# Where the weights lie in SBUF against the activations: a 64-byte gap, and a first chunk split by single row blocks

## The chip, the core and the metric

The kernel runs on one core of one Trainium2 chip, in one launch. The metric is device time in microseconds. Three runs of the kernel before gave 2261.34, 2262.07 and 2262.89 us; the median is 2262.07. All arrays are float32, 517 MB of them pass through the DMA queues, nearly all weights that are read once.

## What is computed

Two transformer blocks on 256 tokens of width 2048, shortened to what fills the time:

```python
# block 1
proj = rms_norm(x, mix_norm) @ w_in                 # 2048 x 5128
h = x + concat([forgetting_attention(q, k, v, log_f), gelu(rg) * rg_lru(conv(rx))]) @ w_out
hn = rms_norm(h, ffn_norm)                          # top-1 group of 4, then top-2 of its 8 experts
for e in range(32):
    out += (silu(hn @ w_gate[e]) * (hn @ w_up[e])) @ w_down[e] * comb[:, e]
h = h + out
h = h + sigmoid(rms_norm(h, ple_norm) @ w_ple_gate) * (p @ w_ple_up)
# block 2
h = h + concat([diff_attention, moba_attention, dilated_attention]) @ w_out_2   # after h @ w_in_2, 2048 x 6144
h = h + memory_cross_attention(rms_norm(h, g_cross), rms_norm(mem, g_mem))
h = h + (silu(conv(rms_norm(h, g_ffn) @ w_up[:, :5632])) * (.. @ w_up[:, 5632:])) @ w_down
return rms_norm(h, g_final)
```

## The kernel before

**Products.** A dense product is computed as three products in the type float32r: weights and activations are each split into a high part (rounded to float32r) and a low part (the rest), and high x high, high x low and low x high are summed in PSUM. `mm` (line 506) issues every one of them. Two forms exist. In `form_a` a 128x128 block of weights is stationary and 256 columns of activations (all tokens) move past it; in `form_b` a 128x128 block of activations is stationary and up to 512 columns of weights move. Form A does `w_in`, `w_out`, the gated per-layer input, `w_in_2`, `w_out_2` and `w_up` (tiles `xth/xtl`, `oth/otl`, `xtph/xtpl`, `xt2h/xt2l`, `ot2h/ot2l`, `xtuh/xtul`, and `xm`, `xtc`, `om` of the memory attention); form B does the values' columns and `w_down` (`hs`).

**The weight stream.** `plan` cuts each weight matrix into units of at most 1 MB, which go by DMA from the SP queue into one of five raw tiles (`raw`). A unit is split in quarters of 1024 columns in a row (`quarters`): ScalarE copies a quarter to a `hi` tile (`split_hi`), VectorE subtracts to a `lo` tile (`split_lo`). There are four `hi` and four `lo` tiles, used in turn; a quarter has its `hi` and its `lo` at the same place in the turn. `next_quarter` takes the next pair, and the loops of `form_a` or `form_b` issue its products: 24 of 256 columns, or 12 of 512. A chunk of 512 output columns is eight quarters. The first chunk (`w_in` from column 3072, 520 wide) differs: a unit there has two row blocks of 520 columns and is one quarter of 1040; its eight columns of the forget gate are a fifth block, so a row block has 15 products and the other blocks start 8 columns into the row.

**The order.** Each engine takes its instructions in the order of emission. Work beside the products (evacuations, attention, norms, splits) is cut into tasks, and a model of the engines' clocks (`clk`, `pump`) picks the step that can start first. It knows no addresses.

**The experts** run on a buffer scheme of their own: their weights are used unsplit, as float32, from raw tiles, from three slots and from the `hi` and `lo` tiles. `gather` (line 1343) multiplies the tokens in rows (`xnh`, `xnl`) by a one-hot tile `gq`; `combine` multiplies the experts' outputs `yy` by a one-hot tile `gt`. Both move the one-hot tile, and both issue 512 products of 256 columns.

**Where tiles lie.** The tile pools are laid one behind the other in a partition in the order in which they are opened, each tile at a multiple of 32 bytes. Before:

| pool | holds | bytes per partition | starts at | modulo 256 |
|---|---|---|---|---|
| `per` | `h`, `ident`, small tiles | 25632 | 16512 | 128 |
| `slots` | six slots: all activation operands | 6 x 16384 | 42144 | 160 |
| `stm` | five `raw` of 8320 | 41600 | 140448 | 160, 32, 160, 32, 160 |
| | four `hi` of 4160 | 16640 | 182048 | 32, 96, 160, 224 |
| | four `lo` of 4160 | 16640 | 198688 | 32, 96, 160, 224 |
| `wk` | six work tiles of 2048, one-hot tiles and `pth`, `ptl` among them | 12288 | 215328 | 32 |
| `sm` | small tiles | | 227616 | |

A tile of 1040 float32 takes 4160 bytes, 64 more than a multiple of 256, so the four `hi` tiles lie at four different residues, and the `lo` tiles at the same four. The allocator hands them out in the order 0, 3, 2, 1, 0, and so on. A row block inside a tile starts a multiple of 512 bytes further (2080 in the first chunk), a block of activations a multiple of 1024: neither changes the residue, but for the first chunk.

Of the kernel before, what the change touches and what calls it, by code (L numbers as in the profile page):

```python
# [30 lines left out]
def block_kernel(ctx: ExitStack, tc: tile.TileContext, A, out, stop=None, dbg=None, force_general=False):  # L31
# [3 lines left out]
    per = ctx.enter_context(tc.tile_pool(name="per", bufs=1))  # L35
    slots = ctx.enter_context(tc.tile_pool(name="slots", bufs=1))
    stm = ctx.enter_context(tc.tile_pool(name="stm", bufs=3))
    wk = ctx.enter_context(tc.tile_pool(name="wk", bufs=1))
    sm = ctx.enter_context(tc.tile_pool(name="sm", bufs=8))
# [7 lines left out]
    # ------------------------------------------------------------------ order of emission  # L47
    # Every engine takes its instructions in the order in which they are emitted. Work beside the matrix products
    # is cut into tasks: generators that name the engine ("a", "d", "p") before each of their steps. A model of
    # the engines' clocks (us) picks the step that can start first, so that no engine waits for another one  # L50
    # inside a chain while it has other work.
# [18 lines left out]
    class Vec:  # L70
        def __getattr__(self, name):
            f = getattr(nc.vector, name)

            def g(o, *a, **k):
                f(o, *a, **k)  # L75
                ins = [x for x in a[:3] if not isinstance(x, (float, int)) and x is not None]
                fast = name in ("tensor_scalar", "tensor_copy", "memset") and all(x.space != PSM for x in ins)
                t = 0.068 + o.free_size() * (0.00052 if fast else 0.00104)
                if name == "tensor_reduce":
                    t = 0.068 + ins[0].free_size() * 0.00104  # L80
                if name in ("tensor_scalar", "scalar_tensor_tensor") and not isinstance(a[1], (float, int)):
                    t += 0.06
                now = clk["d"]
                # an operand that the last instruction has just written costs its latency
                w = last.get("o")
                if o.free_size() <= 64 and any(x.tensor is w for x in ins):
                    t += 0.13
                last["o"] = o.tensor
                clk["d"] = now + t
            return g  # L90
# [4 lines left out]
    def mul(o, l, r, start, stop):  # L95
        """a product beside the stream"""
# [66 lines left out]
    def advance(t):  # L163
        """run the task to its next request; False when it has ended"""
# [17 lines left out]
    def settle(t):  # L182
        """resolve conditions and delays; True when the task asks for an engine"""
# [39 lines left out]
    def candidates(qs):  # L223
        """[(start, priority, run it, engine)]"""
# [16 lines left out]
    def pump():  # L241
        """what fits beside the products that have been emitted"""
# [32 lines left out]
    # ------------------------------------------------------------------ weight stream  # L275
# [74 lines left out]
    for u, un in enumerate(units):  # L350
        if un["kind"] == "dense":
            un["nq"] = max(1, un["nkb"] * un["width"] // 1024)
# [9 lines left out]
    def raw_tile():  # L362
        return stm.tile([128, 4 * 520], F32, name="raw", tag="raw", bufs=RAWS)

    def hl_tiles(dtype):
        return (stm.tile([128, 1040], dtype, name="hi", tag="hi", bufs=HLS),
                stm.tile([128, 1040], dtype, name="lo", tag="lo", bufs=HLS))

    # buffers of the experts' weights: two slots in halves, the raw tiles, the tiles of the split weights, and
    # at first a third slot  # L370
# [13 lines left out]
    def exp_bufs(x):  # L384
        k, i = EBUF[x][0], int(EBUF[x][1])
        if k == "H":
            return [t[:, 0:1024] for t in hl_tiles(F32)], None
        if k == "R":
            t = raw_tile()[:, 0:2048]
# [31 lines left out]
    # the third slot is free after the raw tiles and most of the split weights' that come behind it  # L421
# [12 lines left out]
    def split_steps_open():  # L434
        """the steps of splitting that could be next: [(start, quarter, run it)]"""
# [35 lines left out]
    def next_quarter():  # L471
# [11 lines left out]
        if EXP0 - RAWS <= u < EXP0:  # L483
            # the first of the experts' weights, as tiles get free
# [12 lines left out]
    def need_of(done):  # L497
        """products wait until the blocks up to kb are there"""
# [9 lines left out]
    def form_a(X, kbs, blocks, first, last, need=None, beside=True):  # L508
        """W stationary: blocks = [(psum out [128, S], column, first in its bank)]"""
# [21 lines left out]
    def form_b(X, kbs, banks, first, last, width=512, need=None):  # L531
        """X stationary: banks[tt] psum [128, <=512]"""
# [37 lines left out]
    # ------------------------------------------------------------------ start: loads and constants  # L570
# [13 lines left out]
    # x and the first weights in turns; when they are there, about  # L584
# [16 lines left out]
    def warm(n):  # L601
        """products that nobody reads: the tensor engine's clock rises only after some us of work"""
# [16 lines left out]
    # the other constants, as rows to be transposed  # L619
# [30 lines left out]
    def const_gen():  # L650
# [19 lines left out]
        # half biases of the gates; 2 softplus(-lam), by atanh's series for log1p  # L670
# [37 lines left out]
    # ------------------------------------------------------------------ norms: sums over d, 1/rms per token  # L708
    def rsqrt(n, ssq, scale):
        """[128, n] 1/sqrt(ssq * scale + EPS)"""  # L710
# [18 lines left out]
    def have_r():  # L729
        """the condition that the norm asked for last is there"""  # L730
# [3 lines left out]
    def spread(r):  # L734
        """[128 tok, 2] per-token factors -> [128, 256] on all partitions, in PSUM"""
# [5 lines left out]
    def set_r(ssq, wide):  # L741
        """a task's steps: R["r"] [128 tok, 2] and R["b"] [128, 256] from sums of squares [128 tok, 2]"""
# [32 lines left out]
    def add_sq(sq, t):  # L775
        """the sum of the blocks' squares, by one more"""
# [6 lines left out]
    def operand(dst, kb, gain, sq, t, done):  # L783
        """a task's steps: block kb of h times the gain as an operand, and its squares"""
# [10 lines left out]
    def resid_gen(o, kb, dst, gain, sq, done):  # L795
        """h += o; operand of the next norm"""
# [4 lines left out]
    def split_steps(dst, kb, src, done=None):  # L801
        """a task's steps: an operand of src"""
# [19 lines left out]
    # ================================================================== block 1: mixing  # L822
# [49 lines left out]
    def bias_rows_gen():  # L872
        """relative-position bias of block 2, to DRAM:
        bias_d[head, q, c] = row[head, 127 - q + c], queries 128..255 at keys 0..255"""
# [31 lines left out]
    # minus the sums of log f, in three parts that add up to it exactly, at partitions 0, 32 and 64  # L906
# [61 lines left out]
    def rnn_gen():  # L968
        """scan; rc becomes the state.
        a = exp(-y), s = tanh(y/2): 1/(1+s) = (1+a)/2, refined; a = 2/(1+s) - 1; sqrt(1-a^2) = 2 sqrt(s)/(1+s)"""  # L970
# [27 lines left out]
    # F and RX  # L998
# [17 lines left out]
    # Q, K: per-head norms, transposed  # L1016
# [48 lines left out]
    # attention of block 1  # L1065
    def max_of(srcs, biases, p, m):
        """scores + bias -> p [128, 384], -max in m[2:4]"""
# [13 lines left out]
    def pt_steps(p):  # L1081
        """P [128 q, 384] -> P^T: [128 s0, 256 t] | [128 s1, 128 t]"""
# [11 lines left out]
    def pv_t(t, v, dst, kb, done=None):  # L1094
        """out^T [dh, tok] = V^T P^T, split into dst"""
# [46 lines left out]
    # RG: gelu(rg) * state  # L1142
# [27 lines left out]
    # w_out; tokens in rows for the experts; scores of the router  # L1170
# [33 lines left out]
    def xn_gen(n, tt):  # L1204
# [9 lines left out]
        if n == 3:  # L1214
            # beside the routing on the vector engine
# [46 lines left out]
    # ================================================================== block 1: experts  # L1262
# [22 lines left out]
    # groups of a token: [128, (tt), 4]; experts: [128, (tt, group), 8]. The choice does not depend on the token's  # L1285
    # 1/rms, a positive factor of all its scores; the first of equal ones is taken
# [31 lines left out]
    # place among the expert's tokens from 1 on where selected, 0 elsewhere  # L1318
# [17 lines left out]
    def gather(q):  # L1336
        """the tokens of four experts' slots: xe, by steps of two of its 16 rows"""
# [22 lines left out]
    def weights():  # L1360
        """weights of the two experts, times 1/rms of the token; what goes past the slots"""
# [39 lines left out]
    def loadable(u):  # L1401
        """whether the unit's buffer has been read"""
# [14 lines left out]
    def hidden(i):  # L1417
        """the experts' hidden values of pair i, times the slots' weights, and room for their transpose"""
# [42 lines left out]
    def transposes(i):  # L1461
        """of the hidden values, and of G"""
# [29 lines left out]
    # the first pair's hidden values beside its gather  # L1492
# [13 lines left out]
    for i in range(16):  # L1506
# [7 lines left out]
        if i == 15:  # L1514
            # p^T as an operand
# [9 lines left out]
        for j in range(2):  # L1525
# [16 lines left out]
            if i == 15:  # L1542
                # the next weights are split in time for the products that follow
# [27 lines left out]
    # general path: the tokens past an expert's slots, by dense products over all tokens  # L1571
# [54 lines left out]
    # ================================================================== block 1: gated per-layer input  # L1626
# [52 lines left out]
    # ================================================================== block 2: self attention  # L1679
# [134 lines left out]
    # w_out_2; the memory's operands beside it  # L1814
# [81 lines left out]
    # ================================================================== block 2: memory attention  # L1896
# [98 lines left out]
    # ================================================================== block 2: conv-GLU  # L1995
# [25 lines left out]
    def tok_gen():  # L2021
        """h in place to tokens in rows: h[p, kb, (tt, c)]"""
# [64 lines left out]
    # w_down: hid split as it is used; tokens in rows  # L2087
# [22 lines left out]
    def fin_gen(bank, n, tt):  # L2110
        """h += products (tokens in rows), sums of squares; times the final gain, but for the last columns"""
# [37 lines left out]
    def last_columns(X, banks):  # L2149
        """the last products of the last two column blocks, one token tile after the other"""  # L2150
# [40 lines left out]
def _constants():  # L2191
    """rows of a product with [bias table; ones; dilated heads]: distance d = 255 - i of column i"""
# [42 lines left out]
```

## Time and profile before

| | |
|---|---|
| median of three runs | 2262.07 us |
| profiled execution, span | 2260.5 us |
| TensorE busy | 2210.5 us (98%), 15552 products |
| weight loads of TensorE | 1887.0 us (83%) |
| VectorE busy | 1264.3 us (56%) |
| ScalarE busy | 943.7 us (42%) |
| DMA | 517.30 MB, 229 GB/s over the span, some 400 GB/s in the expert stage |
| granted clock of TensorE | 0.9 or more of full speed in 39 of 40 slices, 0.8 in the other |

The span is the time from the first to the last instruction of the profiled execution; the run's time has a little around it. A product's record is longer (0.28 us for 256 columns) than the distance to the next one's start, since products overlap in the pipeline; the pace of a stream is read from the starts. The stages, in order of time: block 1's mixing to about 395 us, experts to 905, the gated input to 1005, block 2's mixing to 1410, memory attention to 1520, `w_up` to 2005, `w_down` to the end.

### The profile page before, as it was taken

Reading aid. Unit: us, or ns where it says so; the run is one execution under the profiler, and the core shown is the slowest. Engines: PE = TensorE matmul, PEld = TensorE weight load, DVE = VectorE, ACT = ScalarE, POOL = GpSimd, SP = SyncE. Lnnn points to the kernel's source line nnn. Section 1 sums busy time; section 2 is a strip of 40 time slices with the busy share of each in tenths; the row PEclk is TensorE's granted clock in tenths of the full one; section 3 lists DMA queues with packets and bytes.
Section 4 is the critical chain, followed back from the end, with each engine's and each line's share of the span. In section 5 each row is a group of like instructions: output and inputs, shape, how many; then the busy total and the mean of one; then the engine's idle time right before and its main releaser. Section 6 shows DMA issues by size and latency. Waiting matters only on the chain.

```text
span 2260.5 us, 37736 instructions
## 1 busy us (share of the span) xinstructions
PE 2210.5 (98%) x15552; PEld 1887.0 (83%) x15552; DVE 1264.3 (56%) x2251; ACT 943.7 (42%) x1493; POOL 34.0 (2%) x62
## 2 busy tenths in 40 slices
PE   9999979999999999999999999999999999999998
PEld 8888978555455565998999999999999999988886
DVE  8866654233333334875477558675655665564545
ACT  6745533211111112654444446455444444444443
POOL 1000000000000000000000000000000000000000
PEclk9999989999999999999999999999999999999999
DMA  8554668999999997465545556555555565555552
GB/s 282 168 180 164 144 189 304 332 403 396 401 398 396 399 394 276 171 196 194 185 153 170 181 180 192 184 169 170 187 187 188 185 195 191 191 200 193 186 187 93
DMA packets 232415, 517.30 MB, mean 229 GB/s; under 512 B 11783, under 2 KB 51446, under 8 KB 232112
## 3 DMA queue, kind: packets, MB, share of 16 engines
q1 hardware_dynamic: 229168, 506.57, 63.7%
q0 software_dynamic: 3040, 8.27, 1.8%
q8 instruction: 124, 2.03, 0.4%
q14 instruction: 51, 0.42, 0.1%
q10 hardware_dynamic: 32, 0.01, 0.0%
HBM read 510.61 MB, written 4.19 MB: 228 GB/s over the span
## 4 chain that ended last, share of the span: by engine, by line
PE 59%; DVE 0%; ACT 0%; ACTq 0%; issue 0%
PE acc L506 51%; PE sd L506 6%; PE sd L97 2%; PE sd L699 1%; DVE rs L75 0%; DVE hid L75 0%; DVE lo L75 0%; ACT hi L61 0%; ACT junk L61 0%; ACT out L61 0%; DVE h L75 0%; ACT cx L61 0%; DVE hs L75 0%; ACTq L2231 0%; ACT xtph L61 0%
## 5 line engine op out<-in xcount | busy, mean ns | idle before, releaser
L75 DVE TENSOR_TENSOR lo<-raw,hi 128x1024 fp32r<-128x1024 f32 (+1 forms) x572 | 698.6, 1224 | 549.2 <-ACT hi L61 544.1
L61 ACT ACTIVATE hi<-raw 128x1024 fp32r<-128x1024 f32 (+1 forms) x572 | 605.6, 1059 | 768.8 <-PE acc L506 649.2
L506 PE MATMUL acc<-xtuh,hi 128*128 128x256 f32 x1408 | 393.9, 280 | 0.0
L506 PE MATMUL acc<-xtul,hi 128*128 128x256 f32 x1408 | 393.6, 280 | 0.0
L506 PE MATMUL acc<-xtuh,lo 128*128 128x256 f32 x1408 | 393.2, 279 | 0.0
L506 PEld LDWEIGHTS acc<-xtuh,lo 128*128 128x128 f32 x1408 | 266.1, 189 | 0.0
L506 PEld LDWEIGHTS acc<-xtuh,hi 128*128 128x128 f32 x1408 | 266.0, 189 | 0.0
L506 PEld LDWEIGHTS acc<-xtul,hi 128*128 128x128 f32 x1408 | 265.8, 189 | 0.0
L75 DVE TENSOR_TENSOR h<-acc,h 128x512 f32<-128x512 f32 (+1 forms) x180 | 101.7, 613 | 196.0 <-PE acc L506 196.0
L506 PE MATMUL acc<-xt2h,hi 128*128 128x256 f32 x512 | 147.5, 288 | 0.0
L506 PE MATMUL acc<-xt2l,hi 128*128 128x256 f32 x512 | 143.4, 280 | 0.0
L506 PE MATMUL acc<-xt2h,lo 128*128 128x256 f32 x512 | 143.4, 280 | 0.0
L506 PE MATMUL acc<-hi,hs 128*128 128x512 f32 x352 | 112.0, 393 | 0.8 <-ACT hs L61 0.7
L506 PE MATMUL sd<-hi,hs 128*128 128x512 f32 x352 | 111.7, 393 | 0.0
L61 ACT ACTIVATE sg<-acc,ws 128x256 f32<-128x256 f32 x16 | 7.6, 475 | 243.6 <-PE acc L1445 148.2
L506 PEld LDWEIGHTS acc<-xt2h,hi 128*128 128x128 f32 x512 | 96.8, 189 | 4.1 <-issue 4.0
L506 PEld LDWEIGHTS acc<-xt2l,hi 128*128 128x128 f32 x512 | 96.9, 189 | 0.1
L506 PEld LDWEIGHTS acc<-xt2h,lo 128*128 128x128 f32 x512 | 96.7, 189 | 0.0
L75 DVE TENSOR_TENSOR yy<-acc,yy 128x512 fp32r<-128x512 f32 x64 | 44.3, 692 | 92.4 <-ACT yy L61 92.4
L506 PEld LDWEIGHTS acc<-gt,yy 128*128 128x128 f32 x512 | 64.4, 188 | 30.4 <-issue 27.7
L506 PE MATMUL acc<-oth,lo 128*128 128x256 f32 x256 | 72.8, 284 | 12.3 <-DVE lo L75 12.3
L506 PEld LDWEIGHTS acc<-hi,hs 128*128 128x128 f32 x352 | 66.0, 188 | 16.4 <-ACT hs L61 0.9
(390 smaller groups left out, 4711.3 us busy)
## 6 DMA issues: line engine op xcount, KB each, us to landing
raw<-in_w_up_dram SPq DMA_DIRECT2D x88, 1024.0 KB, 5.0
raw<-in_w_in_dram SPq DMA_DIRECT2D x52, 1024.0 KB, 5.2
raw<-in_w_down_dram SPq DMA_DIRECT2D x44, 1024.0 KB, 5.0
raw<-in_w_out_dram SPq DMA_DIRECT2D x32, 1024.0 KB, 5.1
raw<-in_w_in_dram SPq DMA_DIRECT2D x64, 512.0 KB, 4.5
raw<-in_w_expert_down_dram SPq DMA_DIRECT2D x29, 1024.0 KB, 10.1
raw<-in_w_expert_gate_dram SPq DMA_DIRECT2D x45, 512.0 KB, 10.0
raw<-in_w_expert_up_dram SPq DMA_DIRECT2D x45, 512.0 KB, 10.2
```

The source lines that it names most:

```text
L61: nc.scalar.activation(o, i, f, **k)
L75: f(o, *a, **k)
L97: nc.tensor.matmul(o, l, r, start=start, stop=stop, skip_group_check=True)
L506: nc.tensor.matmul(o, l, r, start=first, stop=last, skip_group_check=True)
L699: nc.tensor.transpose(o, i, idt)
```

## The change

Beside the code below, comments and docstrings are taken out and leave empty lines; `HLS` is 4 and `RAWS` 5 in both.

```diff
-    per = ctx.enter_context(tc.tile_pool(name="per", bufs=1))
     slots = ctx.enter_context(tc.tile_pool(name="slots", bufs=1))
     stm = ctx.enter_context(tc.tile_pool(name="stm", bufs=3))
+    gap = ctx.enter_context(tc.tile_pool(name="gap", bufs=1))
+    hlp = ctx.enter_context(tc.tile_pool(name="hlp", bufs=1))
     wk = ctx.enter_context(tc.tile_pool(name="wk", bufs=1))
+    per = ctx.enter_context(tc.tile_pool(name="per", bufs=1))
     sm = ctx.enter_context(tc.tile_pool(name="sm", bufs=8))
...
-            un["nq"] = max(1, un["nkb"] * un["width"] // 1024)
+            un["nq"] = -(-un["nkb"] * un["width"] // 1024)
...
     def raw_tile():
-        return stm.tile([128, 4 * 520], F32, name="raw", tag="raw", bufs=RAWS)
+        return stm.tile([128, 2048], F32, name="raw", tag="raw", bufs=RAWS)
 
     def hl_tiles(dtype):
-        return (stm.tile([128, 1040], dtype, name="hi", tag="hi", bufs=HLS),
-                stm.tile([128, 1040], dtype, name="lo", tag="lo", bufs=HLS))
+        return (hlp.tile([128, 1024], dtype, name="hi", tag="hi", bufs=HLS),
+                hlp.tile([128, 1024], dtype, name="lo", tag="lo", bufs=HLS))
...
         if k == "H":
-            return [t[:, 0:1024] for t in hl_tiles(F32)], None
+            return list(hl_tiles(F32)), None
         if k == "R":
-            t = raw_tile()[:, 0:2048]
+            t = raw_tile()
...
+    nc.gpsimd.memset(gap.tile([128, 16], F32, name="gap"), 0.0)
     h = per.tile([128, KB, S], F32, name="h")
```

Raw tiles shrink from 8320 to 8192 bytes, `hi` and `lo` from 4160 to 4096. The `hi` and `lo` tiles get a pool of their own behind a tile of 64 bytes, the pool `per` moves from the front to behind the work tiles, and the number of quarters of a unit is rounded up instead of down, so that a unit of 2 x 520 columns is split as two quarters of 520 (all other units keep theirs). The slots then start at 16512, 128 modulo 256, and the rest follows from the sizes.

## Rows read from the trace of the kernel before

**Rows 1.** The page, part 1: busy time of each engine, share of the span, instructions.

```profile
PE 2210.5 (98%) x15552; PEld 1887.0 (83%) x15552; DVE 1264.3 (56%) x2251; ACT 943.7 (42%) x1493; POOL 34.0 (2%) x62
```

**Rows 2.** Chain of waits in order of time: start us, us, what.

```profile
1557.90 444.46 PE acc L506 x3815
...
2023.15 11.09 PE acc L506 x48
```

**Rows 3.** Waits of TensorE: who, for whom: us, times, longest.

```profile
PE acc L506 <- DVE lo L75: 12.3, 1, 12.3
```

**Rows 4.** Timeline of TensorE in w_up: start us, us, engine line op out<-in xcount.

```profile
1703.17 0.28 PE L506 MATMUL acc<-xtuh,hi 128*128 128x256 f32 x1
...
1706.01 0.28 PE L506 MATMUL acc<-xtuh,hi 128*128 128x256 f32 x1
...
1706.37 0.28 PE L506 MATMUL acc<-xtuh,hi 128*128 128x256 f32 x1
...
1708.75 0.28 PE L506 MATMUL acc<-xtuh,hi 128*128 128x256 f32 x1
...
1711.63 0.28 PE L506 MATMUL acc<-xtuh,hi 128*128 128x256 f32 x1
...
1714.35 0.28 PE L506 MATMUL acc<-xtuh,hi 128*128 128x256 f32 x1
```

**Rows 5.** Timeline of TensorE, two quarters behind other work, early in w_up.

```profile
1522.64 0.28 PE L506 MATMUL acc<-xtul,hi 128*128 128x256 f32 x1
...
1525.23 0.28 PE L506 MATMUL acc<-xtuh,lo 128*128 128x256 f32 x1
...
1548.91 0.28 PE L506 MATMUL acc<-xtuh,lo 128*128 128x256 f32 x1
...
1550.61 0.28 PE L506 MATMUL acc<-xtuh,lo 128*128 128x256 f32 x1
```

**Rows 6.** Groups of products by operands: xcount | busy us, mean ns | idle.

```profile
L506 PE MATMUL acc<-xtuh,hi 128*128 128x256 f32 x1408 | 393.9, 280 | 0.0
L506 PE MATMUL acc<-xt2h,hi 128*128 128x256 f32 x512 | 147.5, 288 | 0.0
L506 PE MATMUL acc<-hi,hs 128*128 128x512 f32 x352 | 112.0, 393 | 0.8 <-ACT hs L61 0.7
L506 PE MATMUL acc<-xth,hi 128*128 128x256 f32 x272 | 78.0, 287 | 0.0
L506 PE MATMUL acc<-oth,hi 128*128 128x256 f32 x256 | 73.0, 285 | 0.0
```

**Rows 7.** Timeline of TensorE in w_down.

```profile
2103.80 0.63 PE L506 MATMUL sd<-hi,hs 128*128 128x512 f32 x2
...
2105.91 0.63 PE L506 MATMUL sd<-hi,hs 128*128 128x512 f32 x2
...
2109.39 0.62 PE L506 MATMUL sd<-hi,hs 128*128 128x512 f32 x2
...
2111.45 0.39 PE L506 MATMUL sd<-hi,hs 128*128 128x512 f32 x1
```

**Rows 8.** Windows, experts: stretch us, busy PE PEld DVE ACT POOL, clock, DMA share, GB/s.

```profile
600.00:650.00 50.00, 48.69 (x288) 26.23 (x286) 15.47 (x30) 7.48 (x16) 0.00 (x0) 1.00 1.02 396
```

**Rows 9.** Groups of splits and like operations: xcount | busy us, mean ns | idle.

```profile
L61 ACT ACTIVATE hi<-raw 128x1040 fp32r<-128x1040 f32 x8 | 8.7, 1083 | 6.4 <-DMA raw<-in_w_in_dram 5.6 <-PE acc L506 0.8
L61 ACT ACTIVATE yy<-acc 128x512 fp32r<-128x512 f32 x64 | 38.3, 598 | 89.4 <-PE acc L1532 89.4
L75 DVE TENSOR_TENSOR lo<-raw,hi 128x1040 fp32r<-128x1040 f32 x8 | 9.9, 1238 | 3.0 <-ACT hi L61 2.9
L75 DVE TENSOR_TENSOR hs<-hid,hs 128x512 fp32r<-128x512 f32 x22 | 14.8, 685 | 0.6 <-ACT hs L61 0.6
```

**Rows 10.** Timeline of the start, with the idle time before and what ended it.

```profile
9.33 0.39 PE L506 MATMUL acc<-xtl,hi 128*128 128x256 f32 x1 [0.76 <-DVE xtl L75]
```

**Rows 11.** Instructions on the router's weights: duration ns min/median/max, first and last start.

```profile
L1175 POOL DMA_DIRECT2D wr<-in_w_router_expert_dram x1: 1193/1193/1193, 264.1 to 264.1; - x1
```

## The prediction

> **What bounds the kernel now.** I read the busy times first: TensorE is busy 2210.5 of 2260.5 us [rows 1]. Then the chain of waits in order of time: its long pieces are TensorE's own products of line 506, above all one of 444.46 us with 3815 of them in w_up, 116.5 ns from start to start [rows 2]. Nothing else stands in that piece: there the time is the number of products times their pitch. Third, the list of waits: TensorE's longest is a single one of 12.3 us [rows 3], late in block 1's mixing, and against 2260 us it is little. So the question is what sets the pitch.
>
> For that I read the timeline of TensorE alone, product by product, in w_up. Four quarters of a weight chunk follow one another, 24 products each; the rows show the first product of each and of the next turn [rows 4]: 2.84, 2.74, 2.88 and 2.72 us, and then it starts over. Instructions, shapes and granted clock (1.00, so 2.4 GHz) are the same; what has a period of four is the buffer of the split weights. I call *offset* how far the stationary operand lies past the moving one, in bytes modulo 256. Counted in the program's order these quarters lie in weight buffers 0, 3, 2, 1, so at offsets 128, 64, 0 and 192. The pitch is then 118.3, 114.2, 120.0 and 113.3 ns. Within the offset-64 quarter only the first three products are slow (0.36 us, carried over from the quarter before); the other 21 take 2.38 us, 113.4 ns each, as in the offset-192 quarter.
>
> **The layout.** After the change all split weights have one residue. Worked out from tile sizes: the pools lie one behind the other; six slots of 16384 bytes and five raw tiles of 8192 keep the residue, the gap adds 64, eight weight tiles of 4096 keep it. So the split weights, and the work tiles behind them (one-hot tiles among these), lie 64 past the activations in the slots.
>
> *Form A* (weights stationary, 256 columns of activations moving): offset 64 in every quarter. Before, (2.84+2.74+2.88+2.72)/96 = 116.5 ns, the same as in the long piece of the chain. After, 113.4 ns, if the steady pitch of offset 64 lasts. Where other work of TensorE stands before an offset-64 quarter, two steady pitches appear [rows 5]: after a sum of squares the products stay at 117.7 ns (22 in 2.59 us) to the quarter's end; after four transposes they are soon at 113.3 ns (15 in 1.70 us). I went through all 22 offset-64 quarters that begin so: 17 settle at 113 ns, 5 at 117.7. Before, the next quarter's other offset ends either state; after, only an interruption does. So in stages with many interruptions I take 3/4 at 113.4 and 1/4 at 117.7, mean 114.5; the long piece of w_up, uninterrupted for 444 us, takes one of the two as a whole, and I take the commoner.
>
> Counts by line and operand [rows 6], three times each row: w_up 4224; the other stages 3 x (272 + 512 + 256 + two more operands of 256) and 576 in three small ones, 5232, less 240 of the first chunk, where 520-column rows put the blocks at offset 96 and I count no gain: 4992.
> - w_up at 113.4: 4224 x 3.1 ns = -13.1 us. (With the long piece at 117.7: 3815 x 1.2 = +4.6, the rest -1.3.)
> - the others: 4992 x 2.0 = -10.0 us. (All at 113.4: -15.5; all at 117.7: +6.0.)
> - 96 products of p, whose activations lie in work tiles, come to offset 0: 96 x 3.5 ns = +0.3 us.
>
> *Form B* (activations stationary, 512 columns of weights moving). Before, 48 products take 11.09 us, 231.0 ns each [rows 2]. The roles are turned round, so the new layout is offset 192. In w_down nine products at offset 192 take 2.06 us, 228.9 ns each, and at offset 64 2.11 us, 234.4 ns [rows 7]: the sign of the 64 bytes matters here, and it is the cheaper one. 2016 products (1056 in w_down, three times the row in rows 6, and 960 of the same form elsewhere) x 2.1 = -4.2 us.
>
> *Experts.* Gather and combination have 512 products each with a work tile moving: offset 128 before (118.3 ns, as in rows 4), 192 after. Quarters at offset 192 in form A that begin behind other work keep 117.7 ns, all 15 of them, and these groups begin so. I take -0.5 us, between 1024 x 4.9 = -5.0 and 0; the loads run at 396 GB/s with a share of 1.02 there [rows 8], and where they end last the gain is nothing.
>
> The Trainium skill speaks against all this: the page "SBUF — State Buffer", section "Who interferes with whom", says that TensorE never waits for anyone at this memory and has two read ports of its own, one for the moving operand and one for weight loads. By that rule the four quarters would take one time and the layout would be worth nothing. The trace disagrees: 2.72 to 2.88 us for 24 like products [rows 4].
>
> **The first chunk.** Eight units of two row blocks become sixteen quarters of one. ScalarE's split of 1040 columns takes 1.083 us, and 512 columns 0.598, so two of 520 about 1.22: +1.1 us over eight units. VectorE: 1.238 against 2 x 0.685, +1.1 us [rows 9]. A unit's 30 products (3.5 us) hide both, unless a split is late because its load is: then up to 1.1 shows. On the other side TensorE's first products wait 0.76 us for an activation half that stands on VectorE behind the whole first split [rows 10]; half a split ahead of it is 0.55 us shorter, and the same can be won once or twice where a load has just landed. After it x, which comes by DMA, is late next. I take -0.5 us, between -1.5 and +1.5. The gap's memset of 16 columns on GpSimd stands ahead of an iota whose result waits for a load anyway: nothing.
>
> **The stall that stays.** The 12.3 us [rows 3] are VectorE's queue behind the router's weights, whose DMA GpSimd issues at 264.1 us [rows 11] behind transfers that follow TensorE's work. Faster products before it bring the issue forward; the stall moves and keeps its length. Only the last 19 us before it gain nothing, 0.4 us, within the bounds of the start.
>
> **Sum.** -13.1 - 10.0 + 0.3 - 4.2 - 0.5 - 0.5 = -28.0 us on the profiled execution's 2260.5: 2232.5. The median of the runs, 2262.07, is 1.6 above that span: 2234.
>
> **Rivals.**
> - *The long piece settles at 117.7.* For it: both pitches hold for whole quarters, and one interruption decides 444 us. Against: 17 of 22, and 6 of the 7 begun behind transposes of 128 columns, as the long piece is. w_up then costs +3.3 instead of -13.1: 2250.
> - *All fast*, the experts' products too: form A 9216 x 3.1 = -28.6, with form B, p and the start -33.0, with the experts up to -38.0: 2224 to 2229.
> - *Nothing changes*, because the offset only goes along with something else of period four. Against it: the raw tiles have a period of five, and no other buffer that changes by the quarter has four. Only the first chunk is left: 2260.5 to 2263.5.
> - *Slower: the slow pitch everywhere.* A uniform offset keeps 117.7 where the mixture had 116.5: 9216 x 1.2 = +11.1, with form B, p and the start +6.7: 2269. It decides from the share s that settles fast: form A changes by 1.2 (1 - s) - 3.1 s ns a product, and with the rest's -4.4 us the sum turns at s = 0.17. The trace has 0.77.
>
> **Numbers.** Forecast 0.60 (its own range 2227 to 2242), long piece slow 0.22, all fast 0.08, nothing 0.05, slow everywhere 0.05. The range 2223 to 2252 leaves out the last two and the edges. 0.2% is 4.5 us, about what a measurement here can tell from no change. Faster 0.90, same 0.06 (nothing, and part of slow everywhere), slower 0.04.
>
> **What would show it.** Right: four quarters of w_up in 10.9 us instead of 11.18, without period four; the long piece in 432 us; 48 products of w_down in 11.0. First rival: the long piece in 449 us, at 117.7 ns throughout. Wrong altogether: quarters that still differ in turn, or a pitch at offset 64 that is neither of the two; a new wait of TensorE for ScalarE or VectorE in the first 40 us; longer waits in the expert stage.

## The result, and the profile after

The changed kernel takes 2236.11 us (median of 4 runs, 2235.96 to 2236.80), the kernel before 2262.01 in the same job. The ratio is 0.9886, with a 95% interval from 0.9872 to 0.9900: 1.1% faster. The forecast was 2234.0, from 2223 to 2252. The profiled execution's span fell from 2260.5 to 2234.2 us, 26.3 less; the sum had said 28.0.

The busy times of after, the row that answers to [rows 1]. TensorE has as many products as before and is busy 25.7 us less; VectorE and ScalarE have 8 instructions more, the additional splits.

```profile
PE 2184.8 (98%) x15552; PEld 1865.2 (83%) x15552; DVE 1264.2 (57%) x2259; ACT 945.4 (42%) x1501; POOL 34.0 (2%) x63
```

The chain of waits of after, as [rows 2] (start, length, what). The long piece of w_up holds the same 3815 records and lasts 432.41 instead of 444.46 us, 113.3 ns from product to product instead of 116.5. Right ahead of it stand four transposes (`sd L704 x4`). The 48 products of w_down last 10.99 instead of 11.09. The first two pieces are a pair from block 2's mixing: 120 products of one form take 13.62 us in one and 14.14 in the other, so 113.5 and 117.8 ns.

```profile
1237.80 13.62 PE acc L510 x120
...
1263.28 14.14 PE acc L510 x120
...
1545.49 0.44 PE sd L704 x4
1545.92 432.41 PE acc L510 x3815
1998.97 10.99 PE acc L510 x48
```

The span splits at these pieces: the long one starts 11.98 us earlier, is 12.05 us shorter, and from its end to the end of the span the kernel takes 255.9 instead of 258.1 us. These are the 26.3 us.

The timeline of TensorE in w_up of after, as [rows 4], five products that lie 24 apart. From row to row 2.72 us, four times: the period of four is gone, and four quarters take 10.88 us instead of 11.18.

```profile
1690.97 0.28 PE L510 MATMUL acc<-xtuh,hi 128*128 128x256 f32 x1
...
1693.69 0.28 PE L510 MATMUL acc<-xtuh,hi 128*128 128x256 f32 x1
...
1696.41 0.28 PE L510 MATMUL acc<-xtuh,hi 128*128 128x256 f32 x1
...
1699.13 0.28 PE L510 MATMUL acc<-xtuh,hi 128*128 128x256 f32 x1
...
1701.85 0.28 PE L510 MATMUL acc<-xtuh,hi 128*128 128x256 f32 x1
```

The waits of TensorE in after (who, for whom: us, times, longest). The stall of [rows 3] has its old length, 12.1 for 12.3 us. The wait at the start, 0.76 us in [rows 10], is 0.3.

```profile
PE acc L510 <- DVE lo L79: 12.1, 1, 12.1
...
PE acc L510 <- DVE xtl L79: 0.3, 1, 0.3
```

The split of the first chunk in after, as [rows 9] (count | busy, mean ns of one | idle before): 16 pieces of 520 columns cost ScalarE 10.1 us instead of 8.7 and VectorE 10.9 instead of 9.9.

```profile
L79 DVE TENSOR_TENSOR lo<-raw,hi 128x520 fp32r<-128x520 f32 x16 | 10.9, 692 | 2.7 <-ACT hi L65 2.6
L65 ACT ACTIVATE hi<-raw 128x520 fp32r<-128x520 f32 x16 | 10.1, 643 | 9.3 <-DMA raw<-in_w_in_dram 5.6 <-PE acc L510 3.6
```

The expert stage in after, the stretch of [rows 8] (us, busy PE PEld DVE ACT POOL, clock, DMA share, GB/s): no more waiting there, and the loads as full as before.

```profile
600.00:650.00 50.00, 48.69 (x293) 26.82 (x290) 15.42 (x30) 7.35 (x16) 0.00 (x0) 1.00 1.02 398
```

Summed from start to start over the two traces: w_up -12.6 us, the other stages of form A with the first chunk, p and their waits -8.9, form B -3.7, the experts' gather and combination -0.8, all else -0.3.

### The profile page after: what moved, and what is told of

Same layout as the page of the kernel before. It is cut to its first block, busy times and chain, and to the rows that moved or that the text cites. A ratio compares the mean times of both kernels' runs of the same rounds, so it can differ in the third digit from the quotient of the medians.

```text
span 2234.2 us, 37758 instructions
## 1 busy us (share of the span) xinstructions
PE 2184.8 (98%) x15552; PEld 1865.2 (83%) x15552; DVE 1264.2 (57%) x2259; ACT 945.4 (42%) x1501; POOL 34.0 (2%) x63
## 4 chain that ended last, share of the span: by engine, by line
PE 59%; DVE 0%; ACT 0%; ACTq 0%; issue 0%
PE acc L510 51%; PE sd L510 6%; PE sd L101 2%; PE sd L704 1%; DVE rs L79 0%; DVE hid L79 0%; DVE lo L79 0%; ACT hi L65 0%; DVE out L79 0%; ACT out L65 0%; ACT cx L65 0%; DVE h L79 0%; DVE hs L79 0%; ACTq L2236 0%; ACT xtph L65 0%
## 5 line engine op out<-in xcount | busy, mean ns | idle before, releaser
L510 PE MATMUL acc<-xtul,hi 128*128 128x256 f32 x1408 | 389.0, 276 | 0.0
L510 PE MATMUL acc<-oth,lo 128*128 128x256 f32 x256 | 71.9, 281 | 12.1 <-DVE lo L79 12.1
L1450 PE MATMUL acc<-raw,xe 128*64 128x512 f32 x320 | 79.5, 596 | 0.0
```

The lines of the kernel that those rows point to most:

```text
L510: nc.tensor.matmul(o, l, r, start=first, stop=last, skip_group_check=True)
L1450: nc.tensor.matmul(gu[64 * e:64 * e + 64, :], xs, whole.rearrange("p (m k c) -> p m k c", m=2, c=256)[:, :, jj, :], start=f, stop=l, skip_ ...
```

## Experiments

Theory: the offset of the stationary past the moving operand, in bytes modulo 256, sets TensorE's pitch (the time from one product's start to the next one's). Rivals: the smaller splits of the first chunk, the equal residues as such, the tile sizes or pools. Lines are those of the kernel that is edited.

**The first chunk alone** (the kernel before, with one line):

```diff
-            un["nq"] = max(1, un["nkb"] * un["width"] // 1024)
+            un["nq"] = -(-un["nkb"] * un["width"] // 1024)
```

> The kernel before with one edit: the number of quarters of a unit is rounded up, so the first chunk is split by single row blocks; all tiles lie as before. Theory (the offset of the stationary past the moving operand sets the pitch, and the first chunk gives about 0.5 us): 2261.5 us, between 2260.5 and 2263.5, with w_up's 24-product quarters still 2.84, 2.74, 2.88 and 2.72 us in turn. Rival (the smaller splits, not the addresses, bring the gain): about 2236 us.

Measured: 2261.75 us (11 runs) beside 2261.41 of before (15 runs), ratio 1.0000, interval 0.9991 to 1.0009. The chain shows the long piece with its old length, 0.50 us earlier than in [rows 2].

```profile
1557.40 444.46 PE acc L506 x3815
```

The split gives half a microsecond in the one trace, and nothing that the runs can tell from no change. The gain is the layout's.

**The gap at 0, 128 and 192 bytes** (the kernel after, one line each):

```diff
-    nc.gpsimd.memset(gap.tile([128, 16], F32, name="gap"), 0.0)
+                                           # offset 0: line left out
+    nc.gpsimd.memset(gap.tile([128, 32], F32, name="gap"), 0.0)   # offset 128
+    nc.gpsimd.memset(gap.tile([128, 48], F32, name="gap"), 0.0)   # offset 192
```

> The kernel after without the 64-byte gap: every split-weight tile lies at offset 0 to the activations. Theory: form A goes to 120.0 ns and form B to 226.7 ns; 9216 products of form A x (120.0 - 114.5) = +50.7 us, 2016 of form B x (226.7 - 228.9) = -4.4, so 2236 + 46 = 2282 us; slower than the kernel before. Rival (equal residues of all weight tiles bring the gain, whatever the residue): 2236 us. Rival (the address does not matter, only the tile sizes and pools): 2236 us.

> The kernel after with a gap of 128 bytes instead of 64. Theory: form A at 118.4 ns, form B at 232.4; 9216 x 3.9 = +36 us, 2016 x 3.5 = +7 us, so 2279 us. Rival (any offset other than 0 is as good): 2236 us.

> The kernel after with a gap of 192 bytes. Theory, with the sign of the 64 bytes mattering: form A keeps 117.7 ns after every interruption, the whole long piece of w_up too, form B lies at offset 64 and takes 233.3; 9216 x (117.7 - 114.5) = +29.5, 2016 x 4.4 = +8.9, so 2274 us. Rival (a distance of 64 bytes either way is the same, and both pitches occur as at 64): 2236 us for form A, with form B 2245.

Measured: 2281.32 us at 0 (ratio to before 1.0087, interval 1.0072 to 1.0103), 2282.25 at 128 (1.0090, 1.0074 to 1.0105), 2272.52 at 192 (1.0048, 1.0032 to 1.0063). The chains, long piece of w_up and 48 products of w_down, in that order:

```profile
1568.15 460.81 PE acc L510 x3840
...
2242.38 10.88 PE acc L510 x48
```

```profile
1569.10 455.69 PE acc L510 x3840
...
2243.54 11.15 PE acc L510 x48
```

```profile
1560.36 452.28 PE acc L510 x3840
...
2232.28 11.20 PE acc L510 x48
```

Divided: form A takes 120.0, 118.7 and 117.8 ns, form B (whose offset is the negative) 226.7, 232.3 and 233.3. At 128, form A's 118.7 instead of the expected 118.4 makes the kernel 3 us slower than forecast. All three keep the equal residues, sizes, pools and splits of after and are slower than before, so none of the rivals is left: the 64 bytes are the gain. The gap also moves what lies behind it (work tiles, `h`); the streams below leave all of that out. That 192 is not as good as 64 in this program shows that the sign counts. But 192 is not slow by itself: in the kernel before, 39 of 39 quarters at 192 in the long piece took the fast pace (the 2.72 us of [rows 4]), and with 192 everywhere the whole piece takes 117.8 ns. What makes the difference is open: in the streams below, twelve products at offset 0 ahead, as in before, still leave 192 at 117.8. The kernel before was a mixture of four offsets, and its mean lay between the good layout and the bad ones.

**Streams alone.** A kernel with nothing but products on two tiles; its core:

```diff
+    for o in range(0, 64, 4):            # offset in floats
+        cut("T", 4); form_a(o, 48)       # four transposes ahead
+        cut("Q", 2); form_a(o, 48)       # two float32 products of one column
+        form_a(0, 12); form_a(o, 48)
+        cut("T", 4); form_b(o, 24)
+    for o in (16, 48):
+        for kind, n in (("T", 1), ..., ("T", 8), ("Q", 1), ..., ("Q", 8), ("W", 1), ("W", 2)):
+            cut(kind, n); form_a(o, 48)
```

> Leaves out the whole computation: only streams of products on copies of x, with the shapes, the order of operands and the banks of form A and form B. Part 1 takes sixteen offsets in steps of 16 bytes; at each stand 48 products of form A behind four transposes, 48 behind two float32 products of one column, 48 behind twelve products at offset 0, and 24 of form B behind four transposes. Part 2 puts other numbers of transposes and of float32 products ahead of 48 at offsets 64 and 192. Theory (the offset alone sets the pitch): form A 120.0 ns at 0, 113.3 or 117.7 at 64, 118.5 at 128, 117.7 at 192; form B 226.7, 229.0 (at 192 bytes stationary behind), 232.4, 233.3. Within it, on what chooses between 113.3 and 117.7: if the kind of the work before does, transposes lead to 113.3 and one-column products to 117.7 in every repeat; if its length does, the pitch changes with their number. Rival (not the offset, but which pool or buffer of the real kernel, or its DMA writes, set the pitch): one pitch at all sixteen offsets, since here nothing else runs and all operands lie in two tiles.

Measured in one execution, ns from start to start from the ninth product on (form A by what stands ahead; the last column is form B at the offset of the row, behind four transposes):

| offset, bytes | A: 4 transposes | A: 2 columns | A: offset 0 | B |
|---|---|---|---|---|
| 0 | 120.0 | 120.0 | | 226.7 |
| 32 | 118.4 | 118.4 | 118.4 | 233.4 |
| 64 | **113.3** | 117.8 | 117.8 | 233.5 |
| 96 | 117.3 | 117.4 | 117.3 | 234.3 |
| 128 | 118.6 | 118.6 | 118.7 | 232.3 |
| 160 | 120.1 | 119.9 | 119.9 | 233.3 |
| 192 | 117.8 | 117.8 | 117.8 | 228.9 |
| 224 | 116.7 | 116.7 | 116.7 | 233.3 |

The chain, 48 products of form A behind four transposes and 24 of form B; the first two lines belong to offset 0, the other two to weights 64 bytes past the activations (form A's row of 64, form B's row of 192):

```profile
26.87 5.75 PE b L53 x48
...
46.45 5.48 PE b L53 x24
...
128.55 5.46 PE b L53 x48
...
147.64 5.51 PE b L53 x24
```

At the eight offsets between, form A lies from 116.6 (208) to 120.2 and form B from 231.1 to 236.9. So the addresses, together with what stands ahead, are enough to change the pitch, without DMA or other engines at work, and no offset in steps of 16 bytes goes below 113.3. Two steady paces are no peculiarity of 64: behind different work form A runs at 118.3 or 120.0 ns at 16 and at 144, and at 117.3 or 120.0 at 240. In the second part the same 48 products take one of two times (chain, offset 64; L88 are transposes, L53 into `extra` float32 products of one column, two records each; the last two lines are at offset 192):

```profile
443.95 0.33 PE extra L88 x3
444.28 5.46 PE b L53 x48
449.75 0.44 PE extra L88 x4
450.18 5.46 PE b L53 x48
...
467.77 0.87 PE extra L88 x8
468.65 5.66 PE b L53 x48
474.30 0.11 PE extra L53 x2
474.42 5.57 PE b L53 x48
479.99 0.34 PE extra L53 x4
480.33 5.76 PE b L53 x48
486.09 0.56 PE extra L53 x6
486.65 5.57 PE b L53 x48
...
536.04 0.44 PE extra L88 x4
536.48 5.45 PE b L53 x48
```

Offset 64: behind 3 or 4 transposes 5.46 us, behind 8 it is 5.66; behind 1 or 3 columns 5.57 (slow first products, then 113.3 ns), behind 2 it is 5.76. At offset 64 the stretches end at 113.3 ns in 8 of 14 cases, at 192 in 3 of 14, always at one of the two values and to the stretch's end. I had expected the kind of work to decide; it does not, since each kind leads to both, by its number.

**Interruptions put into w_up** (the kernel after; `cut` issues transposes into a bank that nobody reads):

```diff
+    def cut(n):
+        ps = sd()
+        for i in range(n):
+            tp(ps[:, 128 * (i % 4):128 * (i % 4) + 128], h[:, i, 0:128], ident)
     for n in range(11):
+        if n: cut((4, 8)[n % 2])          # run 1: twenty; run 2: only "if n == 1: cut(8)"
         o = chunk_a(X, need_of(xudone) if n == 0 else None)
...
+        if n: cut((3, 2)[n % 2])          # run 1
         o = chunk_a(X)
```

> The kernel after with twenty extra interruptions in w_up: ahead of each of its last twenty chunks of 192 products stand 8, 2, 4, 3 transposes in turn, which nobody reads. They cost 0.88, 0.23, 0.44 and 0.34 us each (length of such transposes in the trace of after plus 0.09 us for the first product behind), 9.5 us in all. Theory (the offset allows two pitches, and what stands before picks one, until the next interruption): chunks behind 4 transposes stay at 113.3 ns, as 18 of 18 stretches do in two traces; behind 3 and behind 8 most go to 117.7 (18 of 22 and 7 of 8 so far), behind 2 unknown. Time 2236.1 + 9.5 + 10 x 192 x 0.84 x 4.4 ns (7.1) = 2252.7 us, up to 2257 if the chunks behind 2 are slow as well. Rival (the whole stage keeps the pace it has, the address alone sets it): all chunks at 113.3, 2245.6 us.

> The kernel after with one extra interruption: eight transposes that nobody reads, ahead of the third chunk of w_up (cost 0.88 us). Theory: this one place decides the 3840 products behind it, which no other work of TensorE interrupts; if it puts them at 117.7 ns (7 of 8 such stretches so far), the long piece is 3840 x 4.4 = 16.9 us longer and the kernel takes 2254 us; if it leaves them at 113.3, 2237. Rival (the pace falls back to 113.3 by itself): 2237 us with a short slow part.

Measured, run 1: 2254.34 us (7 runs, 2251.82 to 2256.22; ratio to before 0.9966, 0.9954 to 0.9977). Its chain, one turn:

```profile
1662.25 0.22 PE sd L704 x2
1662.47 21.78 PE acc L510 x192
1684.25 0.44 PE sd L704 x4
1684.69 21.79 PE acc L510 x192
1706.48 0.33 PE sd L704 x3
1706.80 22.62 PE acc L510 x192
1729.42 0.88 PE sd L704 x8
1730.30 22.61 PE acc L510 x192
```

The chunks here stand behind 2, 4, 3 and 8 transposes. A chunk takes 21.8 us (113.3 ns) behind 4 in five of five cases and 22.6 (117.8) behind 3 in five of five. Behind 8 it is slow in four of four; the earliest of the five eights fell together with four transposes of the kernel's own, and behind these twelve the chunk is fast. Behind 2 the first is slow and the other four fast; the first one followed a fast chunk, the others slow ones, so the pace before may count too, which stays open. The ten slow chunks (10 x 192 x 4.4 ns = 8.4 us) and the transposes' 9.5 make 2254.0.

Run 2: 2236.24 us. The eight again fell together with the four, and behind twelve the long piece stayed at 113.3. So it leaves its question open (whether a slow pace holds for the whole piece), and the next pair put the interruption two chunks later:

```diff
+        if n == 2: cut(3)                 # the other kernel: cut(4)
         o = chunk_a(X, need_of(xudone) if n == 0 else None)
```

> The kernel after with one extra interruption: three transposes that nobody reads, ahead of the fifth chunk of w_up, inside the long piece (the eight of the run before fell together with four others and made twelve). Cost 0.34 us. Theory: three leave the products behind them at 117.7 ns, as in five of five places of the run with twenty interruptions, and nothing ends that before the end of w_up; 3456 products x 4.4 ns = 15.4, with the transposes 15.7 us: 2252 us. Rival (the pace comes back to 113.3 by itself, or the slow chunks of the run before came from the repeated interruptions): 2236.5 us.

> The same place with four transposes instead of three, one product of 128 columns more. Cost 0.44 us. Theory: four leave the products at 113.3 ns (five of five): 2236.6 us, 15 us less than with three. Rival (any interruption at this place slows what is behind it): 2252 us.

Measured: 2251.96 us with three (4 runs, 2250.57 to 2253.19; ratio 0.9954, 0.9937 to 0.9971) and 2236.81 with four (4 runs, 2235.89 to 2237.43; 0.9890, 0.9873 to 0.9906). The chains, three first:

```profile
1547.48 43.55 PE acc L510 x384
1591.03 0.33 PE sd L704 x3
1591.36 407.05 PE acc L510 x3456
```

```profile
1545.38 43.55 PE acc L510 x384
1588.93 0.44 PE sd L704 x4
1589.37 388.89 PE acc L510 x3431
```

A third of a microsecond of work costs 15 us behind it: 117.8 ns a product to the end of w_up, 407 us later. One transpose more avoids it. The two kernels' runs do not overlap.

**A version ahead of both** (the kernel after): w_down's split hidden values 64 bytes further, so that form B comes to offset 0.

```diff
-    hs = [slot(i, [128, 2, 2, 4, S], F32R, f"hs{i}") for i in (2, 3)]
+    hs = [slot(i, [128, 4096], F32R, f"hs{i}")[:, 16:3088].rearrange("p (g k s) -> p g k s", g=3, k=4)
+          for i in (2, 3)]
...
-        return hs[(g % 4) // 2][:, g % 2, 0], hs[(g % 4) // 2][:, g % 2, 1]
+        return hs[0][:, g % 3], hs[1][:, g % 3]
```

> The kernel after with one edit: w_down's split hidden values lie 64 bytes further, so that in w_down both operands have the same residue (three groups in turn instead of four). Theory: 48 products of w_down take 10.88 us instead of 10.99, 22 such groups, -2.4 us: 2233.7 us. Rival (a turn of three holds up the splits or the products): 2236 us or more. Rival (w_down's pitch hangs on something other than its operands' addresses): 2236 us.

Measured: 2233.26 us (4 runs, 2232.41 to 2235.37), ratio to before 0.9871, interval 0.9854 to 0.9887. The interval overlaps that of after; the chain shows the step that was meant, 10.88 for 10.99 us, and 22 of them make 2.4 us.

```profile
2174.64 10.88 PE acc L510 x48
```

## Why the prediction was right, and where it was off

- *Form A in w_up*, -13.1 predicted, -12.6 measured. Long piece 432 predicted, 432.41 measured. Which pace the piece would take was a bet on counts (17 of 22, and 6 of 7 behind transposes of 128 columns): the prediction did not know what chooses. The pair with three and four transposes shows that 15 us hung on it. Behind four transposes of 128 columns, as ahead of this piece, 18 of 18 stretches in the traces of after and of the version ahead of both run at 113.3; at its very start only twelve were tried beside four, and they left it fast too.
- *Form A elsewhere*, 4992 x 2.0 = -10.0 predicted, -9.0 measured. This term was mis-sized. In steady running the pitch went from 116.95 to 115.41 ns, where 116.5 and 114.5 were taken: some 4800 distances x 1.54 = -7.4. Of 4804 products in settled stretches 57% run at 113.3 and 43% at 117.7, where 3/4 and 1/4 were taken. Shorter waits and fewer slow first products, which the sum did not have, add -1.6. The share came from counting 22 quarters of before as equals. Only 7 of them stood behind transposes of 128 columns, and 8, all fast, behind one kind of work (score products, `qk`); in after a stretch keeps its pace to its end, so that long ones weigh most, and three of these (240, 288 and 312 products, from block 2's `w_out_2` to the start of w_up) ran at 117.8. The share is not fixed by the layout either: in the traces of the five kernels that equal after up to w_up, a like count gives 48 to 54% fast.
- *p*, +0.3 predicted: its 96 products went from 117.4 to 119.4 ns, +0.2.
- *Form B*, -4.2 predicted, -3.7 measured. In w_down 10.99 us for 48, as forecast.
- *Experts*, -0.5 predicted, -0.8 measured, all of it in the gather, without a new wait. *Start*: -0.5 predicted; the long piece began 0.50 us earlier in the trace of the kernel with that edit alone. The stall kept its length, as said.
- *Rivals.* Long piece slow: 2250 forecast; three transposes made nine tenths of it slow, 2251.96. Slow everywhere: 2269 forecast; the gap of 192 bytes is that case, 2272.52, with form B at 233.3 ns on top. All fast did not come: 43% of the other products stayed slow, some 2070 x 4.4 ns = 9.1 us. No kernel was run that speeds these up; an extra four transposes cost 0.44 us, more than a stretch of under 100 products gives back (an estimate, 100 x 4.4 ns).
- *Nothing changes*: this would also have come of a rule of the Trainium skill, "SBUF — State Buffer", section "Who interferes with whom", that TensorE never waits for anyone at this memory. The runs here contradict it for TensorE's own two operands: one gap of 64 bytes more or less moves the kernel from 2236 to 2281 us with the same instructions.
- The sum, -28.0, missed by 1.7 us in the span: the share cost 2.6, of which 1.6 came back as said, w_up and form B gave 0.5 less each, and small terms make up the rest. The runs of after lie 1.9 us above the span instead of 1.6. That the total came so close is in part luck, since the 1.6 us were not foreseen.
- Why the offset changes the pitch, and why it allows two, no run here shows.

## What to carry to other kernels

Where a stream of TensorE's products ends last, read its pitch from starts, buffer by buffer: a period equal to the number of buffers points at their addresses. Give all buffers of a turn one residue and choose it by measurement for each form, since a uniform bad residue (2281 us) is worse than a mixture (2262). Then look at what stands ahead of each long stretch: a small interruption can set the pace of thousands of products behind it.

## What the runs showed that I had not expected

- At offsets 64 and 192 two steady pitches exist, 113.3 and 117.8 ns, and a stretch keeps its own for 400 us. Other offsets have pairs of their own.
- Which one comes hangs on the number of transposes or columns ahead, but not on it alone: at 64 three transposes lead to 113.3 ns in the stream kernel and to 117.8 in w_up, and at 192 four lead to 113.3 in the stream kernel and to 117.8 ahead of w_up's long piece. What else counts is open. It is mostly the same from run to run: between the traces of after and of the version ahead of both, the same program up to w_down, some 8300 of 9000 products of form A lie in stretches of equal pace, some 700 do not.
- The two forms want different offsets: 64 is the best for form A and costs form B 233.5 ns, 0 is the best for form B (226.7) and gives form A 120.0. A gap can serve both only because the roles, and so the sign, are turned round between them, or by moving one operand for one stage, as in the last kernel.
